# Branch projections run together after the attention, and an output projection with seven of eight half products

## The chip, the cores and the metric

The kernel runs on one core of one Trainium2 chip. The metric is the device time of one execution in microseconds (us). Engines are named as in the profile: PE (TensorE, matmuls), PEld (its weight loads), DVE (VectorE), ACT (ScalarE), POOL (GpSimd) and SP (SyncE, which issues most DMAs). Each engine works its own list in order.

## What is computed

One layer of a streaming encoder on T = 1152 tokens (1024 of a prompt, 128 of eight running streams). An input projection feeds an mLSTM branch and an attention branch. The stretch that is changed is the end of the layer:

```
def merge_out(x, h_m, mz, h_a, az, gm, ga, w_bm, w_ba, w_out):
    u_m = jnp.einsum("btc,cd->btd", h_m * jax.nn.silu(mz), w_bm)
    u_a = jnp.einsum("btc,cd->btd", h_a * jax.nn.silu(az), w_ba)
    mix = jax.nn.sigmoid(gm) * u_m + jax.nn.sigmoid(ga) * u_a
    return x + jnp.einsum("btd,de->bte", mix, w_out)
```

`h_m` and `h_a` are 512 wide, `mix` and the output 1024 wide. All of it is float32.

## The kernel before

Activations lie feature by token: 128 features on the partitions, tokens along the free axis. A float32 product is made of three fp32r matmuls: an operand is split into `hi` (ACT copies it, rounding) and `lo` (the rest, by a subtraction on DVE or POOL; `split`, L98 to L100), and `mm3` (L113 to L116) adds hi·hi, hi·lo and lo·hi into one bank of PSUM. Every matmul loads its own 128x128 weights. `load_nt` (L102) fetches 128 output features' weights in parts of four 128x128 blocks, 256 KB each, into `wr` (2 buffers), and splits them into `wh` and `wl` (3 buffers each).

A planner (`run_line`) interleaves attention chains with input projection tiles; a compile-time scheduler fixes the order on every engine. When the tiles run out, `um_work` does the mLSTM branch: `load_ops` brings `h_m·silu(mz)` back from DRAM (`hm_sc`) into rows 0 to 3 of `h_hi` and `h_lo`, which held the layer's input; then eight output tiles of three chunks of 384 tokens, 12 matmuls each, into `pmain` (2 banks). Their evacuation (`um_evac`) loads the gate from `tg_sc`, multiplies on DVE and stores to `sm_sc`. `load_ops(o_sc, 4)` then fills rows 4 to 7 with the attention's output. The branch from `w_ba` follows, again eight tiles of three chunks (6 banks): DVE multiplies by the gate, POOL adds the stored mLSTM part (L982), and the sum is split into `x_hi` and `x_lo`. At last eight output tiles of three chunks, 24 matmuls each, are added to x (L995) and stored. The three stages have 288, 288 and 576 matmuls of 384 columns.

Of the kernel before, what the change touches and what calls it, by code (L numbers as in the profile page):

```python
# [26 lines left out]
KSC = float(P ** -0.5)  # L27


def emit(tc, a, o, ctx):  # L30
# [930 lines left out]
    load_ops(o_sc, 4)  # L961
# [10 lines left out]
    for j in range(8):

        sa = f(wq_.tile([P, KD, CH], F32R, tag=("w_hi", "w_lo")[j % 2], name="sa", bufs=1)).rearrange("p k c -> p (k c)")
        sm, ta = sa[:, 0:T], sa[:, T:2 * T]
        sp.dma_start(sm, sm_sc[j])
        sp.dma_start(ta, tg_sc[8 + j])

        def ev_a(c, ps):
            s = slice(c * CH, (c + 1) * CH)  # L980
# [6 lines left out]
    def x_rhs(k, c):  # L987
        s = slice(c * CH, (c + 1) * CH)
        return x_hi[:, k, s], x_lo[:, k, s]

    for e in range(8):
        def ev(c, ps):
            xr = wq_.tile([P, CH], F32, tag="wqr", name="xr", bufs=4).rearrange("p (i t) -> p i t", i=3)
# [116 lines left out]
```

## Time and profile before

| | us |
|---|---|
| median of 3 runs (1068.13 to 1069.43) | 1068.95 |
| the profiled execution | 1067.38 |
| its span | 1065.6 |
| PE busy in the span | 1052.3 |
| DVE busy | 657.4 |
| ACT busy | 421.4 |
| POOL busy | 242.5 |

A matmul's duration in the trace is longer than the distance to the next one's start, since matmuls overlap in the array; what a stream of matmuls costs is read from the starts. The granted TensorE clock is full in all slices but the last. HBM moved 122 GB/s over the span.

### The profile page before, as it was taken

How to read it: one execution, taken by the hardware profiler on the slowest of the kernel's cores; microseconds unless marked ns; L12 is line 12 of the kernel's file. 1: busy time of each engine (PE TensorE's matmuls, PEld its weight loads, DVE VectorE, ACT ScalarE, POOL GpSimd, SP SyncE). 2: the span in 40 equal slices, each digit the busy share in tenths (PEclk: the TensorE clock that was granted, in tenths of full speed). 3: DMA queues.
4: the chain of work that ended last, by engine and by line, in shares of the span. 5: the costliest groups of instructions: out<-in, count | busy, mean ns of one | idle time of the engine just before them, and what ended most of it. 6: DMA issues, size and time to landing. Idle time of an engine off the chain costs nothing.

```text
span 1065.6 us, 19714 instructions
## 1 busy us (share of the span) xinstructions
PE 1052.3 (99%) x7078; PEld 1023.0 (96%) x7078; DVE 657.4 (62%) x1931; ACT 421.4 (40%) x976; POOL 242.5 (23%) x406
## 2 busy tenths in 40 slices
PE   7999999999999999999999999999999999999998
PEld 6999999999999999999999999999999999999998
DVE  6745234856747678877877788878753253664221
ACT  6443343344443224654455545545454330231100
POOL 3000000201102234333433344334322000351000
PEclk9999999999999999999999999999999999999999
DMA  8544333452634353423342244123322388663442
GB/s 225 172 90 80 123 49 65 90 119 78 121 105 147 122 181 125 138 67 99 127 139 76 84 132 147 48 83 123 112 87 82 112 267 248 190 221 116 142 139 67
DMA packets 115664, 131.58 MB, mean 123 GB/s; under 512 B 28197, under 2 KB 91885, under 8 KB 115566
## 3 DMA queue, kind: packets, MB, share of 16 engines
q1 hardware_dynamic: 108654, 120.88, 39.6%
q10 hardware_dynamic: 6912, 9.44, 2.4%
q8 instruction: 56, 0.92, 0.4%
q14 instruction: 42, 0.34, 0.1%
HBM read 96.84 MB, written 33.44 MB: 122 GB/s over the span
## 4 chain that ended last, share of the span: by engine, by line
PE 88%; DMA 5%; DVE 4%; issue 1%; ACT 1%; POOL 1%; SPq 0%; DVEq 0%; POOLq 0%; ACTq 0%
PE pm L114 24%; PE pm L116 23%; PE pm L115 23%; PE pT L571 3%; PE pv L733 3%; DMA sm_sc<-tm 1%; PE pS L703 1%; PE pS L704 1%; DMA xt<-in_x 1%; PE pv L817 1%; PE pv L115 1%; PE pv L116 1%; PE pv L114 1%; DMA V<-v_sc 1%; PE pS L792 1%
## 5 line engine op out<-in xcount | busy, mean ns | idle before, releaser
L114 PE MATMUL pm<-h_hi,wh 128*128 128x384 f32 x1056 | 357.3, 339 | 1.9 <-DVE tm L905 1.1
L116 PE MATMUL pm<-h_hi,wl 128*128 128x384 f32 x1056 | 357.6, 339 | 0.0
L115 PE MATMUL pm<-h_lo,wh 128*128 128x384 f32 x1056 | 357.0, 338 | 0.0
L114 PEld LDWEIGHTS pm<-h_hi,wh 128*128 128x128 f32 x1056 | 198.4, 188 | 6.2 <-issue 3.1
L116 PEld LDWEIGHTS pm<-h_hi,wl 128*128 128x128 f32 x1056 | 198.4, 188 | 1.5
L115 PEld LDWEIGHTS pm<-h_lo,wh 128*128 128x128 f32 x1056 | 198.5, 188 | 0.6
L99 ACT ACTIVATE wh<-wr 128x512 fp32r<-128x512 f32 x104 | 65.1, 628 | 166.6 <-PE pm L115 142.2
L114 PE MATMUL pm<-w_hi,h_hi 128*128 128x384 f32 (+1 forms) x360 | 121.1, 337 | 3.1 <-ACT h_hi L99 1.8
L116 PE MATMUL pm<-w_hi,h_lo 128*128 128x384 f32 (+1 forms) x360 | 119.0, 332 | 1.2 <-DVE h_lo L100 1.2
L115 PE MATMUL pm<-w_lo,h_hi 128*128 128x384 f32 (+1 forms) x360 | 118.8, 331 | 0.0
L100 DVE TENSOR_TENSOR wl<-wr,wh 128x512 fp32r<-128x512 f32 x100 | 76.9, 769 | 67.6 <-ACT wh L99 67.5
L563 ACT ACTIVATE prob<-prob,mx 128x640 f32<-128x640 f32 (+4 forms) x72 | 51.2, 711 | 85.6 <-DVE mx L562 63.6
L565 POOL TENSOR_SCALAR prob<-prob,mx 128x640 f32<-128x640 f32 (+4 forms) x72 | 50.7, 704 | 149.0 <-DVE mx L564 88.1
L114 PEld LDWEIGHTS pm<-w_hi,h_hi 128*128 128x128 f32 x360 | 68.3, 190 | 7.7 <-issue 4.1
L116 PEld LDWEIGHTS pm<-w_hi,h_lo 128*128 128x128 f32 x360 | 68.0, 189 | 2.7 <-DVE h_lo L100 1.7
L115 PEld LDWEIGHTS pm<-w_lo,h_hi 128*128 128x128 f32 x360 | 68.2, 190 | 0.1
L114 PE MATMUL pm<-x_hi,wh 128*128 128x384 f32 x192 | 65.0, 339 | 0.0
L116 PE MATMUL pm<-x_hi,wl 128*128 128x384 f32 x192 | 65.0, 339 | 0.0
L115 PE MATMUL pm<-x_lo,wh 128*128 128x384 f32 x192 | 65.0, 338 | 0.0
L560 DVE CUSTOM_DVE_ANT_0 prob<-pS,bias 128x640 f32<-128x640 f32 (+4 forms) x64 | 41.8, 653 | 17.2 <-PE pT L571 8.6
L982 POOL TENSOR_TENSOR sa<-sa 128x384 f32<-128x384 f32 x24 | 27.7, 1163 | 108.3 <-DVE sa L981 108.3
L995 DVE SCALAR_TENSOR_TENSOR xr<-pm,xr 128x384 f32<-128x384 f32 x24 | 13.4, 558 | 59.4 <-PE pm L116 59.4
(220 smaller groups left out, 1782.1 us busy)
## 6 DMA issues: line engine op xcount, KB each, us to landing
wr<-in_wn SPq DMA_DIRECT2D x72, 256.0 KB, 3.0
tg_sc<-tg SPq DMA_DIRECT2D x48, 192.0 KB, 1.9
kr<-in_Kc SPq DMA_DIRECT2D x16, 512.0 KB, 5.3
vr<-in_Vc SPq DMA_DIRECT2D x16, 512.0 KB, 5.2
wqr<-in_wq SPq DMA_DIRECT2D x32, 192.0 KB, 3.3
xt<-in_x SPq DMA_DIRECT2D x9, 512.0 KB, 5.5
tm<-tg_sc SPq DMA_DIRECT2D x24, 192.0 KB, 2.9
sa<-tg_sc SPq DMA_DIRECT2D x8, 576.0 KB, 5.2
```

The source lines that it names most:

```text
L99: act.activation(out=hi, in_=raw, func=AF.Copy)
L100: eng.tensor_tensor(out=lo, in0=raw, in1=f(hi), op=ALU.subtract)
L114: mm(ps, lhs[0], rhs[0], start=first, stop=False)
L115: mm(ps, lhs[0], rhs[1], start=False, stop=False)
L116: mm(ps, lhs[1], rhs[0], start=False, stop=last)
L560: dve.tensor_tensor_reduce(out=view, in0=pS, in1=bias, scale=1.0, scalar=-3e38, op0=ALU.add, op1=ALU.max, accum_out=mx[:, 0:1])
L563: act.activation(out=pt[:, :nk], in_=pt[:, :nk], func=AF.Exp, bias=mx[:, 1:2], accum_out=mx[:, 2:3])
L565: pool.tensor_scalar(out=pt[:, :nk], in0=pt[:, :nk], scalar1=mx[:, 3:4], scalar2=1.0, op0=ALU.mult, op1=ALU.mult)
L571: pe.transpose(pT[:, n * P:(n + 1) * P], pt[:, n * P:(n + 1) * P], ident)
L733: mm(pv[:, j * 256:(j + 1) * 256], at("Vst")[:, i + 1 - nb + n, j, :], st[:, n].rearrange("p a q -> p (a q)"), start=n == 0, stop=n == nb - 1)
L982: pool.tensor_tensor(out=sm[:, s], in0=sm[:, s], in1=ta[:, s], op=ALU.add)
L995: dve.scalar_tensor_tensor(out=xr, in0=ps.rearrange("p (i t) -> p i t", i=3), scalar=0.5, in1=xr, op0=ALU.mult, op1=ALU.add)
```

## The change

The mLSTM branch leaves the planner. Once the planner is done, both operands are loaded by quarters of 288 tokens (`HC`; a half `HF` is 576), part s = 0 of both halves first, then s = 1. For each s and each of four steps `jj`, the two branches are made for output features `jj` and `jj + 4` and both halves: four tiles of `w_bm` weights and products into `pmain`, then of `w_ba` into six banks, eight products of 12 matmuls a step. There is no `sm_sc` any more. `lo` of the weights is made on POOL. From the four results r11, r21, r12, r22 (feature half, token half) the step makes seven operands, x11, x22, x12 and four sums, and splits each.

The output projection takes output tiles in pairs. The weights of a pair are four blocks, b11, b12, b21, b22, from which seven operands are made as well. Seven products of 4·3 matmuls for each s give four blocks of outputs (Winograd's form), where eight would be needed directly. The three running sums of a part stand in three PSUM banks. Split weights lie in columns of `h_hi` and `h_lo` that the s = 1 products have read; four of the s = 1 operands in columns that the s = 0 products have read. Matmuls in the three stages: 384, 384 and 672, of 288 columns.

```diff
@@ -880,31 +883,14 @@
-    def um_work():
-        load_ops(hm_sc, 0)
-        for j in range(8):
-            w = load_nt(a["wbm"][j], 4)
-            for c in range(NCH):
-                yield from chunk(c, w, h_rhs, um_evac(j), 4)
...
+    def load_ops(src, k0, s):
+        for half in range(2):
+            t = slice(half * HF + s * HC, half * HF + (s + 1) * HC)
...
-            t_ = wq_.tile([P, CH], F32, tag="wqr", name="tm", bufs=4)
-            sp.dma_start(t_, tg_sc[j][:, s])
-            dve.scalar_tensor_tensor(out=t_, in0=t_, scalar=1.0, in1=ps, op0=ALU.add, op1=ALU.mult)
-            act.dma_start(sm_sc[j][:, s], t_)
-        return ev
+                raw = spl.tile([P, 1024], F32, tag="kvr", name="raw", bufs=4)[:, 0:2 * HC].rearrange("p (k t) -> p k t", k=2)
+                sp.dma_start(raw, src[kk:kk + 2, :, t].rearrange("k p t -> p k t"))
+                split(h_hi[:, k0 + kk:k0 + kk + 2, t], h_lo[:, k0 + kk:k0 + kk + 2, t], raw)
...
-            if not did and not work and ums is not None:
-                if next(ums, "end") == "end":
-                    ums = None
-                else:
-                    line.now += 480
-                did = True
...
-    load_ops(o_sc, 4)
+    for s in range(2):
+        load_ops(hm_sc, 0, s)
+        load_ops(o_sc, 4, s)
...
-    for j in range(8):
-        sa = f(wq_.tile([P, KD, CH], F32R, tag=("w_hi", "w_lo")[j % 2], name="sa", bufs=1)).rearrange("p k c -> p (k c)")
-        sm, ta = sa[:, 0:T], sa[:, T:2 * T]
-        sp.dma_start(sm, sm_sc[j])
-        sp.dma_start(ta, tg_sc[8 + j])
-        def ev_a(c, ps):
-            s = slice(c * CH, (c + 1) * CH)
-            dve.scalar_tensor_tensor(out=ta[:, s], in0=ta[:, s], scalar=1.0, in1=ps, op0=ALU.add, op1=ALU.mult)
-            pool.tensor_tensor(out=sm[:, s], in0=sm[:, s], in1=ta[:, s], op=ALU.add)
-            split(x_hi[:, j, s], x_lo[:, j, s], sm[:, s])
-        feature_tile(load_nt(a["wba"][j], 4), lambda k, c: h_rhs(4 + k, c), ev_a, 4, pp, "pu")
...
-        def ev(c, ps):
-            xr = wq_.tile([P, CH], F32, tag="wqr", name="xr", bufs=4).rearrange("p (i t) -> p i t", i=3)
-            sp.dma_start(xr, a["xT"][3 * c:3 * c + 3, :, e, :].rearrange("i p t -> p i t"))
-            dve.scalar_tensor_tensor(out=xr, in0=ps.rearrange("p (i t) -> p i t", i=3), scalar=0.5, in1=xr, op0=ALU.mult, op1=ALU.add)
-            act.dma_start(o["y"][e][:, c * CH:(c + 1) * CH], xr.rearrange("p i t -> p (i t)"))
-        feature_tile(load_nt(a["wout"][e]), x_rhs, ev, KD, pp, "pu")
...
+    names = ("x11", "S1", "x12", "S2", "S4", "S3", "x22")
+    X_ = {}
+    for s in range(2):
+        for q, n_ in enumerate(names):
+            if s == 1 and q < 4:
+                k0, t0 = KH * (q // 2), HF * (q % 2)
+                X_[n_, s] = [t_[:, k0:k0 + KH, t0:t0 + HC] for t_ in (h_hi, h_lo)]
+            else:
+                X_[n_, s] = [fp.tile([P, KH, HC], F32R, name=f"{n_}_{s}_{r_}") for r_ in ("hi", "lo")]
...
+        return pp.tile([P, 512], F32, tag="b" + "350214"[(Bank.n - 1) % 6], name="pu")[:, :HC]
+    def branch(ps, w, k0, half, s):
+        t = slice(half * HF + s * HC, half * HF + (s + 1) * HC)
+        for k in range(KH):
+            mm3(ps, w[k], (h_hi[:, k0 + k, t], h_lo[:, k0 + k, t]), k == 0, k == KH - 1)
+    for s in range(2):
+        c = slice(s * HC, (s + 1) * HC)
+        for jj in range(KH):
+            tm, ta = ([sap.tile([P, 2, HC], F32, tag=f"{t_}{e}", name=t_, bufs=2 if t_ == "tm" else 1) for e in range(2)] for t_ in ("tm", "ta"))
+            for t_, j0, e in ((tm, 0, 1), (tm, 0, 0), (ta, 8, 0), (ta, 8, 1)):
+                sp.dma_start(t_[e], tg_sc[j0 + jj + KH * e].rearrange("p (h t) -> p h t", h=2)[:, :, c])
+            for e in (1, 0):
+                w = load_nt(a["wbm"][jj + KH * e], 4, eng=pool)
+                for half in range(2):
+                    ps = pmain.tile([P, 512], F32, tag="pm", name="pm")[:, :HC]
+                    branch(ps, w, 0, half, s)
+                    x = tm[e][:, half, :]
+                    dve.scalar_tensor_tensor(out=x, in0=x, scalar=1.0, in1=ps, op0=ALU.add, op1=ALU.mult)
+            r = {}
+            for e in (0, 1):
+                w = load_nt(a["wba"][jj + KH * e], 4, eng=pool)
+                for half in ((0, 1) if e == 0 else (1, 0)):
+                    ps = bank()
+                    branch(ps, w, KH, half, s)
+                    x, t_ = tm[e][:, half, :], ta[e][:, half, :]
+                    if e:
+                        dve.scalar_tensor_tensor(out=ps, in0=t_, scalar=1.0, in1=ps, op0=ALU.add, op1=ALU.mult)
+                        dve.tensor_tensor(out=ps, in0=ps, in1=x, op=ALU.add)
+                        r[half] = ps
+                    else:
+                        dve.scalar_tensor_tensor(out=t_, in0=t_, scalar=1.0, in1=ps, op0=ALU.add, op1=ALU.mult)
+                        pool.tensor_tensor(out=x, in0=x, in1=t_, op=ALU.add)
+            r11, r21, r12, r22 = tm[0][:, 0, :], tm[0][:, 1, :], r[0], r[1]
+            t3, t2 = (stg.tile([P, CH], F32, tag="th", name=n_)[:, :HC] for n_ in ("t3", "t2"))
+            def put(n_, raw, eng=dve):
+                q = X_[n_, s]
+                split(q[0][:, jj, :], q[1][:, jj, :], raw, eng)
+            put("x11", r11, pool)
+            pool.tensor_tensor(out=t3, in0=r11, in1=r21, op=ALU.subtract)
+            put("S3", t3, pool)
+            put("x22", r22)
+            dve.tensor_tensor(out=r22, in0=r22, in1=r21, op=ALU.add)
+            put("S1", r22)
+            dve.tensor_tensor(out=t2, in0=r22, in1=r11, op=ALU.subtract)
+            put("x12", r12)
+            dve.tensor_tensor(out=r12, in0=r12, in1=t2, op=ALU.subtract)
+            put("S4", r12)
+            put("S2", t2, pool)
+    views = [[t_[:, k0:k0 + KH, t0:t0 + P] for t_ in (h_hi, h_lo)] for k0 in (0, KH) for t0 in (HC, HC + P, HF + HC, HF + HC + P)]
...
+    def w_raw():
+        raws[0] += 1
+        q = raws[0] % 5
+        if q in (1, 4):
+            return wp.tile([P, 4, P], F32, tag="wr", bufs=2, name="wr").rearrange("p k c -> p (k c)")
+        return sap.tile([P, 512 if q == 2 else 2 * HC], F32, tag={2: "wr", 3: "ta0", 0: "ta1"}[q], name="wr", bufs=1)[:, 0:512]
+    def product(ps, w, x, first):
+        for k in range(KH):
+            for l, r in ((0, 0), (0, 1), (1, 0)):
+                mm(ps, w[l][:, k, :], x[r][:, k, :], start=first and k + l + r == 0, stop=k == KH - 1 and l == 1, skip_group_check=True)
...
+        def halves(x):
+            hi, lo = views[parts[0] % len(views)]
+            parts[0] += 1
+            split(hi, lo, x.rearrange("p (k c) -> p k c", k=KH))
+            return hi, lo
...
+        w = {}
+        b11, b12 = load(n1, 0), load(n2, 0)
+        w[1] = halves(b11)
+        b21, b22 = load(n1, 1), load(n2, 1)
+        sub(b11, b12, b11)
+        w[5] = halves(b11)
+        w[2] = halves(b21)
+        t2 = w_raw()
+        sub(t2, b22, b11)
+        w[6] = halves(t2)
+        w[3] = halves(b22)
+        sub(b12, b22, b12)
+        w[7] = halves(b12)
+        sub(b21, b21, t2)
+        w[4] = halves(b21)
+        def steps(s):
+            X, W, Z = (pp.tile([P, 512], F32, tag=banks[2 * q + s], name="py")[:, :HC] for q in range(3))
+            (p1, t_), (u2, xr) = ([t[:, q, :] for q in range(2)] for t in (sap.tile([P, 2, HC], F32, tag=n_, name=n_) for n_ in ("tm0", "tm1")))
+            product(X, w[1], X_["x11", s], True)
+            act.activation(out=p1, in_=X, func=AF.Copy)
+            yield
+            product(W, w[5], X_["S1", s], True)
+            act.activation(out=t_, in_=W, func=AF.Copy)
+            pool.tensor_tensor(out=t_, in0=p1, in1=t_, op=ALU.add)
+            yield
+            product(X, w[2], X_["x12", s], False)
+            out(0, 0, s, X)
+            yield
+            product(Z, w[6], X_["S2", s], True)
+            add(dve, u2, Z, p1)
+            yield
+            product(W, w[3], X_["S4", s], False)
+            add(dve, u2, W, u2)
+            out(1, 0, s, u2)
+            yield
+            product(Z, w[7], X_["S3", s], False)
+            add(dve, t_, Z, t_)
+            out(1, 1, s, t_, xr)
+            yield
+            product(Z, w[4], X_["x22", s], False)
+            add(dve, p1, Z, p1)
+            out(0, 1, s, p1)
...
+    for n1 in range(0, 8, 2):
+        s0, s1 = out_pair(n1, n1 + 1)
+        next(s0)
+        if left:
+            next(left, None)
+        order = (s0,) * 5 + (s1, s0) + (s1,) * 5 if n1 < 6 else (s0, s0) + (s1, s0) * 4 + (s1,) * 5
+        for th in order:
+            next(th, None)
+        left = s1
+    next(left, None)
...
-    d["xT"] = c(xa.reshape(NT, P, KD, P).transpose(0, 3, 2, 1))
+    d["xT"] = c(xa.T).reshape(KD, P, T)
```

PE, where the last gate tile (`pm_10433`) ends and the branches begin. Before:

```order
L116 MATMUL pm_10433<-h_hi_89,wl_10374 128x384
L114 MATMUL pm_10491<-h_hi_89,wh_10487 128x384
L115 MATMUL pm_10491<-h_lo_90,wh_10487 128x384
L116 MATMUL pm_10491<-h_hi_89,wl_10488 128x384
...
L116 MATMUL pm_10491<-h_hi_89,wl_10488 128x384
L114 MATMUL pm_10508<-h_hi_89,wh_10487 128x384
L115 MATMUL pm_10508<-h_lo_90,wh_10487 128x384
L116 MATMUL pm_10508<-h_hi_89,wl_10488 128x384
```

and now (`pm` is the product of `w_bm`, `pu` that of `w_ba`; line numbers are three higher):

```order
L119 MATMUL pm_10433<-h_hi_89,wl_10374 128x384
L117 MATMUL pm_10573<-h_hi_89,wh_10569 128x288
L118 MATMUL pm_10573<-h_lo_90,wh_10569 128x288
L119 MATMUL pm_10573<-h_hi_89,wl_10570 128x288
...
L119 MATMUL pm_10573<-h_hi_89,wl_10570 128x288
L117 MATMUL pu_10641<-h_hi_89,wh_10637 128x288
L118 MATMUL pu_10641<-h_lo_90,wh_10637 128x288
L117 MATMUL pu_10656<-h_hi_89,wh_10637 128x288
L118 MATMUL pu_10656<-h_lo_90,wh_10637 128x288
L117 MATMUL pm_10587<-h_hi_89,wh_10569 128x288
...
L119 MATMUL pu_10641<-h_hi_89,wl_10638 128x288
```

Before, the next 12 matmuls use the same weights `wh_10487`. Now four matmuls on the attention's operand, with weights `wh_10637`, stand between the first and the second product of `w_bm`, and the rest of the product `pu_10641` comes after the second.

ACT at the same place (`tg` is a gate's evacuation, `raw` a loaded piece of an operand). Before:

```order
L201 ACTIVATE tg_10402<-pm_10377,bh_88 128x384
L99 ACTIVATE h_hi_89<-raw_10469 128x2x384
L99 ACTIVATE h_hi_89<-raw_10473 128x2x384
L201 ACTIVATE tg_10430<-pm_10405,bh_88 128x384
L99 ACTIVATE h_hi_89<-raw_10477 128x2x384
L99 ACTIVATE h_hi_89<-raw_10941 128x2x384
L99 ACTIVATE wh_10544<-wr_10542 128x512
L99 ACTIVATE h_hi_89<-raw_10481 128x2x384
L99 ACTIVATE h_hi_89<-raw_10945 128x2x384
L99 ACTIVATE wh_10601<-wr_10599 128x512
L201 ACTIVATE tg_10458<-pm_10433,bh_88 128x384
```

and now:

```order
L204 ACTIVATE tg_10402<-pm_10377,bh_88 128x384
L102 ACTIVATE h_hi_89<-raw_10477 128x2x288
L102 ACTIVATE h_hi_89<-raw_10481 128x2x288
L204 ACTIVATE tg_10430<-pm_10405,bh_88 128x384
L102 ACTIVATE h_hi_89<-raw_10469 128x2x288
L102 ACTIVATE wh_10603<-wr_10601 128x512
L102 ACTIVATE h_hi_89<-raw_10473 128x2x288
L102 ACTIVATE h_hi_89<-raw_10485 128x2x288
L102 ACTIVATE wh_10637<-wr_10635 128x512
L204 ACTIVATE tg_10458<-pm_10433,bh_88 128x384
L102 ACTIVATE h_hi_89<-raw_10489 128x2x288
```

Before, six pieces of the attention's output and of `h_m` are mixed, with the two next weights ahead of the last gate `tg_10458`. Now the piece `raw_10485`, the seventh to be loaded into four buffers, stands ahead of the weights `wh_10637` and of `tg_10458`.

POOL after the attention. Before (the last row of the attention and the first tiles of the `w_ba` stage):

```order
L747 TENSOR_TENSOR ot_10119<-ot_10119,za_4167 128x128
L982 TENSOR_TENSOR sa_10977<-sa_10977 128x384 x3
L982 TENSOR_TENSOR sa_11037<-sa_11037 128x384 x3
L982 TENSOR_TENSOR sa_11097<-sa_11097 128x384 x3
L982 TENSOR_TENSOR sa_11157<-sa_11157 128x384 x3
```

and now, in the first two steps (`L1012` adds the branches, `L1021` is r11 - r21, `L103` makes the `lo` of weights and operands):

```order
L1012 TENSOR_TENSOR tm_10559<-tm_10559,ta_10561 128x288
L103 TENSOR_TENSOR wl_10738<-wr_10735,wh_10737 128x512
L1012 TENSOR_TENSOR tm_10559<-tm_10559,ta_10561 128x288
L103 TENSOR_TENSOR wl_10772<-wr_10769,wh_10771 128x512
L1021 TENSOR_TENSOR t3_10707<-tm_10559 128x288
L103 TENSOR_TENSOR x11_0_lo_10540<-tm_10559,x11_0_hi_10539 128x288
L103 TENSOR_TENSOR wl_10806<-wr_10803,wh_10805 128x512
L103 TENSOR_TENSOR S3_0_lo_10550<-t3_10707,S3_0_hi_10549 128x288
L103 TENSOR_TENSOR wl_10842<-wr_10839,wh_10841 128x512
L103 TENSOR_TENSOR S2_0_lo_10546<-t2_10708,S2_0_hi_10545 128x288
```

Before, POOL has three additions a tile and nothing else. Now each step gives it four `lo` of weights and six operations on operands, in one list.

## Rows read from the trace of the kernel before

**Rows 1.** The page: busy time by engine, and the chain that ended last by engine.
```profile
PE 1052.3 (99%) x7078; PEld 1023.0 (96%) x7078; DVE 657.4 (62%) x1931; ACT 421.4 (40%) x976; POOL 242.5 (23%) x406
...
PE 88%; DMA 5%; DVE 4%; issue 1%; ACT 1%; POOL 1%; SPq 0%; DVEq 0%; POOLq 0%; ACTq 0%
```

**Rows 2.** Busy time by stretch; the header names the columns.
```profile
core 0: us, PE busy (x) PEld busy (x) DVE busy (x) ACT busy (x) POOL busy (x), PEclk, DMA share, GB/s
857.46:865.00 7.54, 6.80 (x39) 6.48 (x39) 6.64 (x9) 5.13 (x8) 0.00 (x0) 1.00 0.90 260
865.00:886.00 21.00, 19.92 (x112) 18.93 (x111) 8.52 (x14) 3.22 (x6) 0.00 (x0) 1.00 0.84 279
886.00:960.28 74.28, 74.28 (x431) 74.28 (x429) 42.15 (x66) 17.64 (x33) 24.26 (x21) 1.00 0.67 214
960.28:1062.20 101.92, 101.92 (x577) 101.59 (x576) 26.80 (x44) 10.31 (x17) 3.44 (x3) 1.00 0.37 117
```

**Rows 3.** Timeline of PE at the first branch products: start, duration, instruction, [idle before].
```profile
857.46 0.33 PE L114 MATMUL pm<-h_hi,wh 128*128 128x384 f32 x1
...
860.44 0.45 PE L114 MATMUL pm<-h_hi,wh 128*128 128x384 f32 x1 [0.74 <-ACT tg L201]
```

**Rows 4.** Timeline of the last microseconds, PE and DVE.
```profile
1061.86 0.34 PE L116 MATMUL pm<-x_hi,wl 128*128 128x384 f32 x1
...
1062.24 0.56 DVE L995 SCALAR_TENSOR_TENSOR xr<-pm,xr 128x384 f32<-128x384 f32 x1 [3.68 <-PE pm L116]
```

**Rows 5.** Timeline of PE: first and last starts of three unbroken streams.
```profile
27.10 0.28 PE L114 MATMUL pm<-w_hi,h_hi 128*128 128x264 f32 x1
...
31.11 0.28 PE L114 MATMUL pm<-w_hi,h_hi 128*128 128x264 f32 x1
...
774.51 0.31 PE L703 MATMUL pS<-Kst,q_hi 128*128 128x320 f32 x1
...
774.95 0.31 PE L704 MATMUL pS<-Kst,q_lo 128*128 128x320 f32 x1
...
886.44 0.33 PE L114 MATMUL pm<-h_hi,wh 128*128 128x384 f32 x1
...
899.96 0.33 PE L114 MATMUL pm<-h_hi,wh 128*128 128x384 f32 x1
```

**Rows 6.** Operand loads: timelines of SP and ACT, and the loads' time to landing.
```profile
848.08 1.41 SPq L896 DMA_DIRECT2D raw<-hm_sc  x2
...
854.54 0.85 ACT L99 ACTIVATE h_hi<-raw 128x768 fp32r<-128x768 f32 x1 [0.41 <-PE pm L116]
856.57 0.85 ACT L99 ACTIVATE h_hi<-raw 128x768 fp32r<-128x768 f32 x1 [1.18 <-DMA raw<-o_sc]
...
DMA to landing us min/median/max: 4.2/4.5/5.9
```

**Rows 7.** POOL: additions L982 (min/median/max ns), and two subtractions by form.
```profile
L982 POOL TENSOR_TENSOR sa<-sa x24: 1004/1207/1517, 908.0 to 964.2; 128x384 f32<-128x384 f32 x24
...
L100 POOL TENSOR_TENSOR w_lo<-wqr,w_hi 128x264 fp32r<-128x264 f32 x8 | 5.8, 748 | 13.0 <-ACT w_hi L99 12.9
...
L100 POOL TENSOR_TENSOR wl<-wr,wh 128x512 fp32r<-128x512 f32 x4 | 5.1, 1291 | 9.0 <-ACT wh L99 9.0
```

**Rows 8.** Groups by form, DVE and ACT: busy us, mean ns of one | idle before.
```profile
L100 DVE TENSOR_TENSOR wl<-wr,wh 128x512 fp32r<-128x512 f32 x100 | 76.9, 769 | 67.6 <-ACT wh L99 67.5
L100 DVE TENSOR_TENSOR x_lo<-sa,x_hi 128x384 fp32r<-128x384 f32 x24 | 15.5, 647 | 7.8 <-ACT x_hi L99 7.7
L905 DVE SCALAR_TENSOR_TENSOR tm<-tm,pm 128x384 f32<-128x384 f32 x24 | 13.3, 553 | 28.9 <-DMA tm<-tg_sc 11.8 <-PE pm L116 11.6 <-DMA sm_sc<-tm 3.2
...
L99 ACT ACTIVATE wh<-wr 128x512 fp32r<-128x512 f32 x104 | 65.1, 628 | 166.6 <-PE pm L115 142.2 <-DMA tm<-tg_sc 7.1 <-DMA wr<-in_wbm 6.2
```

**Rows 9.** DMA issues from 830 us: count, KB each, median us to landing.
```profile
wr<-in_wbm SPq DMA_DIRECT2D x8, 256.0 KB, 5.1
wr<-in_wba SPq DMA_DIRECT2D x8, 256.0 KB, 3.5
```

More of the change, by code (lines that the diff above doesn't have):

```diff
@@ L27 @@
 KSC = float(P ** -0.5)
+HF = T // 2
+HC = HF // 2
+KH = KD // 2
 def emit(tc, a, o, ctx):
@@ L915, in run_line @@
         pairs = pair_work()
-        ums = um_work()
         work = {"pairs": pairs, "tiles": tile_work()}
@@ L947, in run_line @@
                         break
-            if not did and not work and ums is not None:
-                if next(ums, "end") == "end":
-                    ums = None
-                else:
-                    line.now += 480
-                did = True
             if not did:
-                if not live and not samples and not work and ums is None:
+                if not live and not samples and not work:
                     break
@@ L987, in x_rhs @@
[L987 to L992, printed above, removed]
-            xr = wq_.tile([P, CH], F32, tag="wqr", name="xr", bufs=4).rearrange("p (i t) -> p i t", i=3)
-            sp.dma_start(xr, a["xT"][3 * c:3 * c + 3, :, e, :].rearrange("i p t -> p i t"))
-            dve.scalar_tensor_tensor(out=xr, in0=ps.rearrange("p (i t) -> p i t", i=3), scalar=0.5, in1=xr, op0=ALU.mult, op1=ALU.add)
-            act.dma_start(o["y"][e][:, c * CH:(c + 1) * CH], xr.rearrange("p i t -> p (i t)"))
-        feature_tile(load_nt(a["wout"][e]), x_rhs, ev, KD, pp, "pu")
+    esQ.close()
@@ new lines, in emit @@
+    esA, sap = open_pool("sa", bufs=2, side="right")
+    esF, fp = open_pool("fin", side="right")
+    esPS, pp = open_pool("pF", space=PSUM)
+    names = ("x11", "S1", "x12", "S2", "S4", "S3", "x22")
[7 more added lines that the diff above has]
+                X_[n_, s] = [fp.tile([P, KH, HC], F32R, name=f"{n_}_{s}_{r_}") for r_ in ("hi", "lo")]
@@ new lines, in emit, with bank @@
+    banks = [f"b{q}" for q in range(6)]
+    class Bank:
+        n = 0
+    def bank():
+        Bank.n += 1
+        return pp.tile([P, 512], F32, tag="b" + "350214"[(Bank.n - 1) % 6], name="pu")[:, :HC]
[46 more added lines that the diff above has]
+            put("S2", t2, pool)
@@ new lines, in add, with out_pair, load, sub @@
+    def add(eng, out, x, y):
+        eng.tensor_tensor(out=out, in0=x, in1=y, op=ALU.add)
+    def out_pair(n1, n2):
+        def load(n, q):
+            t_ = w_raw()
+            sp.dma_start(t_, a["wout"][n][:, KH * q:KH * q + KH, :].rearrange("p k c -> p (k c)"))
+            return t_
+        def halves(x):
[3 more added lines that the diff above has]
+            return hi, lo
+        def sub(out, x, y):
+            pool.tensor_tensor(out=out, in0=x, in1=y, op=ALU.subtract)
+        def out(e, half, s, x, xr=None):
+            n, c = (n1, n2)[e], slice(half * HF + s * HC, half * HF + (s + 1) * HC)
+            if xr is None:
+                outs[0] += 1
+                q = outs[0] % 3
+                xr = stg.tile([P, CH], F32, tag="gz" if q == 2 else "th", name="xr", bufs=1 if q == 2 else 2)[:, :HC]
+            sp.dma_start(xr, a["xT"][n][:, c])
+            dve.scalar_tensor_tensor(out=xr, in0=x, scalar=0.5, in1=xr, op0=ALU.mult, op1=ALU.add)
+            act.dma_start(o["y"][n][:, c], xr)
+        w = {}
[40 more added lines that the diff above has]
+            out(0, 1, s, p1)
+        return steps(0), steps(1)
@@ L999, in emit @@
+    left = None
+    for n1 in range(0, 8, 2):
[8 more added lines that the diff above has]
+    next(left, None)
     esPS.close()
     esF.close()
-    esQ.close()
+    esA.close()
 def layout(x):
```

14 lines of the change are left out of this document (2 added, 12 removed).

## The prediction

> **What bounds the kernel.** I read the page first. PE is busy for 1052.3 us, 99% of the span, and the chain that ended last is 88% PE [rows 1]: time goes away only if PE has less to do, or comes back as gaps on PE. The windows come next, with the change's place cut out by stages [rows 2]. In the timeline the first `w_bm` matmul starts at 857.46 [rows 3] and the last of all at 1061.86 [rows 4]; with one matmul's distance it is done at 1062.04, 204.6 us later. On PE's list nothing ahead of 857.46 is changed. The granted clock is 1.00 in all four windows, 2.4 GHz.
>
> The stretch has 1152 matmuls of 384 columns. In the `w_ba` stage 78 start-to-start distances take 899.96 - 886.44 = 13.52 us, .1733 each [rows 5]. The output window has 577 in 101.92, .1766 each, and no idle time. The two branches take 960.28 - 857.46 = 102.82 for 576 (99.8 at .1733), so they lose 3.0; of it (7.54 - 6.80) + (21.00 - 19.92) = 1.82 shows as idle PE [rows 2], the rest as slower starts around the gaps. So today's stretch is nearly dense too.
>
> **What the change does to PE.** There are 384 + 384 + 672 = 1440 matmuls of 288 columns: 1440 x 288 = 414,720 columns for 442,368, 6.25% fewer, yet 288 instructions more. The distance at 288 isn't in the trace. Its neighbours are .1215 at 264 (4.01 us over 33) and .1733 at 384 [rows 5]; the line between them gives .1319. Scaling the output window's .1766 by 288/384 gives .1325, and that I take, since it holds the small losses of a real stage. Low bound: .130, proportional to .1733. High bound: .134, a little above 264's .1215 scaled by 288/264 (.1326). (The 320-column products, .147, are three distances of a short burst, for a rival.) PE then needs 187.2, 190.8 or 193.0 us, against 204.6 now: 13.8 us less before any wait.
>
> **What is removed and added on other engines.** The mLSTM part is no longer stored and loaded back, but each branch weight now comes twice, 32 tiles for 16. A branch step, 96 x .1325 = 12.7 us of PE, brings four weight tiles of 256 KB and four gate tiles of 295 KB, 2.2 MB or 174 GB/s, less than the 214 of 886 to 960 [rows 2]. POOL gets, per step, four `lo` of weights at 1.29 and six operations of 288 columns. For these, 264 columns take .748 and the quickest 384-column addition 1.004 [rows 7], so .80; together 10.0 us. A 384-column addition took 1.207 in the median; if all ran 20% longer POOL would need 12.0, still under 12.7. DVE has 13 operations a step with PSUM or two operands at about .45 (three quarters of .553, and a little) and four `lo` of operands at .49 (three quarters of .647) [rows 8], 7.8 us. ACT has four `hi` of weights at .63 and seven of operands below that, at most 6.9. No engine but PE fills a step. Cover for POOL's work is the next weights being wanted a step later; it is thin, and a rival below.
>
> In the output stage a pair is 168 matmuls, 22.3 us. DVE makes seven `lo` of weights (7 x .77) and some 16 operations of about .45, 12.6; POOL some 7. Both hide.
>
> **The waits that it adds on PE**, in order of place.
>
> *The start, 3.0.* The second group on PE needs `wh_10637`, the first `w_ba` weights. On ACT these stand behind `raw_10485`, the seventh piece into four buffers. Its load can go out only when the split of the piece that held its buffer before, `raw_10469`, is done. ACT's copy of that one stands right behind the gate `tg_10430`, as the copy at 854.54 does now [rows 6]; it takes .64 (three quarters of .85), and DVE's `lo` after it ends near 856.1. Such loads need 4.2 to 5.9 to land [rows 6], so 860.3 to 862.0; `hi` .65 and `wh` .63 [rows 8] make 861.4 to 863.1. PE has one product, 12 x .1325 = 1.6, from 857.46 to 859.05: it waits 2.4 to 4.1. I take 3.0. Behind ACT's wait stand the gate `tg_10458` and the later copies, which nobody wants sooner. Now PE loses .74 at the like place [rows 3].
>
> *The next loads, .7.* The pieces for s = 1 and two more weights pass through the same SP queue in the first step, where today's windows move 260 and 279 GB/s [rows 2]. Below: 0; above: the 1.8 that idles now.
>
> *Branch to output, .5.* Of the first pair's four weight blocks the third (b21) goes into the place of a gate (`ta0`) that is free only after POOL's last addition from it, and lands, at 3.5 [rows 9], 2.5 to 3.3 us into the output stage. With its copy and `lo` it is ready at about 4.8 to 5; PE first does three products, 4.75, so 0 to .5.
>
> *The last pair, .8.* Its final two products share one bank. The last can begin when DVE has added the one before (about .45 and the signalling); everywhere else another part's product fills that place.
>
> *Slow starts after gaps, 1.2*, as 3.0 - 1.82 today.
>
> **The sum.** 857.46 + 190.8 + 3.0 + .7 + .5 + .8 + 1.2 = 1054.5, against 1062.04: -7.6. Behind the last matmul comes today one DVE operation of .56 [rows 4] and a store; then two, the shorter one each, +.3. So -7.3 on a profiled execution of 1067.38, which is 1.57 below the median: 1060.1 there, **1061.6 as a median**. By the bounds (-3.6 and +2.2 on the matmuls, -1.5 and +1.5 on the waits) 1056.5 to 1065.3.
>
> **The rivals.**
>
> *Waits that hide (.12).* The matmuls run proportionally and half the waits vanish: -3.6 - 2: 1055 to 1058. For it: ACT and DVE have time. Against: the output window has no gap and still runs at .1766.
>
> *Late weights, mild (.13).* Only two buffers take raw weights. The second `w_ba` tile of a step can be issued only when the `lo` of a tile two earlier is done on POOL, at best 8.3 us into the step; with .7 for its predecessor's copy ahead of it, 1.3 for that `lo`, 3.5 landing and signalling [rows 9], and .7, it is there at 14.7 counted from the step's start, and PE wants it at 12.7 + 3.2 = 15.8: 1.1 to spare. At 5.1, as `w_bm` loads take at 260 to 279 GB/s, it is .5 late, and so is the following step's first: 1 us a step, seven steps, +7, 1065 to 1071, with 1068.6 at its middle. Against: the stage asks for 174 GB/s, and at 214 landing was 3.5.
>
> *Late weights, severe (.07): slower.* The same place: the delay grows by 2 x 7 = 14 us per us of landing beyond 4.6. At 5.1 the saving of 7.3 is gone; from 5.27 the kernel is slower by more than 2.1 us. The longest landing seen, 5.9 [rows 6], gives +18, 1080. POOL slowed as its longest addition (1517 for 1004 [rows 7]) acts alike: 10.0 x 1.5 = 15 us a step for 12.7, +2.3 in each of eight steps, 1080. The Trainium skill, "GPSIMD Engine Reference", section "1. Specifications", says that GpSimd shares its interfaces to SBUF with VectorE. The spread of POOL's additions agrees; in the new stage most of DVE's operations read PSUM, which speaks for less of it.
>
> *A fixed cost per matmul (.03): slower.* If much of the .1733 did not shrink with the columns, more and shorter matmuls would cost time: the saving ends at (204.6 - 6.5) / 1440 = .1376. At 320's .147 [rows 5] PE would need 211.7, +20.9, 1082. The 33 distances of .1215 at 264 columns, with the same three forms and weight loads, nearly rule it out. The Trainium skill, "TensorE: Matmul & The Clock Gate", section "Back-to-back issue gap", gives some 81 ns at 128 columns and 131 at 512 for pairs of weight load and matmul; an estimate by it would be 102 at 288 and 114 at 384, hence 146.7 us for 131.6, a loss of 15 us. Rows 5 show distances that go with the columns, and the measurement decides.
>
> *Something unseen (.05)*, half of it on either side: the start costs 6 or more, or the scheduler's order starves PE in the output stage (the weights' `lo` and the evacuations are in one DVE list).
>
> **Chances.** My own case, 1058 to 1065.5, has .60. What a measurement of this kernel tells from no change is .2%, 2.1 us: below 1066.8 is faster, above 1071.1 slower. Faster: .60 + .12 + .05 of the mild case + .02 = .79. Same: .08 + .01 = .09. Slower: .07 + .03 + .02 = .12. The range leaves out the ends: 1056 to 1070.
>
> **What the profile will show.** Matmul starts .1325 apart in dense pieces of both stages (.130 or .134 at the bounds; .14 or more is the fixed cost). One gap of 2.4 to 4.1 near 859, ended by ACT's `wh`. Eight steps in 101.8 plus about 5, so the output stage from about 965; its end at 1054 to 1055. In the steps, gaps on PE ahead of a first matmul of a weight tile, ended by `wh` or `wl`, mean late weights; then POOL's share of a step or the landing of `wr` says which of the two. A long row of DVE releases in the output stage means that the sharing of banks costs more than the one .8. I am wrong above all if POOL's `lo` of weights take 1.7 or more, or the loads land above 4.6.

## The result, and the profile after

The changed kernel takes 1059.76 us (median of 4 runs, 1058.85 to 1062.8), before 1069.19: a ratio of .9918, interval .9895 to .994, so 9.4 us less. Five more runs of the same kernel (`e0_again`) gave 1060.77 beside 1069.12 for before, ratio .992 (.9907 to .9932). Forecast were 1061.6, within 1056 to 1070. The profiled execution took 1058.85, 8.5 less than that of before, where -7.3 was forecast.

The page, first and chain lines, to stand beside [rows 1]:

```profile
PE 1042.3 (99%) x7366; PEld 1012.9 (96%) x7366; DVE 688.0 (65%) x2035; ACT 452.9 (43%) x1056; POOL 324.0 (31%) x486
...
PE 89%; DMA 5%; DVE 3%; ACT 1%; issue 1%; POOL 1%; SPq 0%; POOLq 0%; ACTq 0%; DVEq 0%
```

PE has 10 us less to do with 288 matmuls more. The windows, cut where the branches begin, where the gaps end, and where the output begins (as [rows 2]):

```profile
859.61:880.00 20.39, 19.81 (x148) 19.34 (x148) 16.37 (x31) 12.18 (x23) 13.17 (x12) 1.00 0.82 243
880.00:962.48 82.48, 82.48 (x624) 82.48 (x623) 45.55 (x110) 32.28 (x70) 64.15 (x66) 1.00 0.56 166
962.48:1053.02 90.54, 89.72 (x674) 89.18 (x672) 53.57 (x97) 23.30 (x48) 29.48 (x26) 1.00 0.46 138
```

The branches take 962.48 - 859.61 = 102.87, as before (102.82). The output takes 90.54 for 101.76. The gain is all in the output projection; the stretch is 193.4 for 204.6. Inside the branches two differences cancel: 768 distances of .1327 (below) are 101.9 us, where 576 of .1733 [rows 5] were 99.8, so the same columns cost 2.1 us more, and what is lost in gaps is 1.0 for 3.0.

The timeline of PE: the first matmul, the gaps, the first and last start of the longest unbroken stream, and the last product:

```profile
859.61 0.29 PE L117 MATMUL pm<-h_hi,wh 128*128 128x288 f32 x1
...
875.80 0.40 PE L117 MATMUL pu<-h_hi,wh 128*128 128x288 f32 x1 [0.22 <-ACT wh L102]
...
876.95 0.40 PE L117 MATMUL pm<-h_hi,wh 128*128 128x288 f32 x1 [0.35 <-DVE tm L997]
...
877.44 0.30 PE L117 MATMUL pm<-h_hi,wh 128*128 128x288 f32 x1
...
962.35 0.30 PE L119 MATMUL pu<-h_hi,wl 128*128 128x288 f32 x1
962.48 0.29 PE L1048 MATMUL py<-x_hi,h_hi 128*128 128x288 f32 x1
...
1051.32 0.40 PE L1048 MATMUL py<-x_hi,h_hi 128*128 128x288 f32 x1 [0.62 <-DVE tm L1051]
...
1052.88 0.29 PE L1048 MATMUL py<-x_hi,h_lo 128*128 128x288 f32 x1
```

From 877.44 to 962.35 there are 640 distances: 84.91 / 640 = .1327. One reads the cost of a gap from the starts around it, not from the idle in brackets: 875.28 to 875.80 is .52, so .39 more than a distance, and the next distance is .24.

Ahead of the branches the changed kernel is 2.15 us later (859.61 for 857.46). This part does the same work in both kernels. Two gaps stand there that the first profile of before doesn't have, on instructions that are the same in both:

```profile
235.86 0.44 PE L117 MATMUL pm<-h_hi,wh 128*128 128x384 f32 x1 [0.91 <-ACT go L335]
...
283.91 0.44 PE L119 MATMUL pm<-h_hi,wl 128*128 128x384 f32 x1 [1.04 <-DVE wl L103]
```

The sum, forecast against profile:

| | forecast | profile |
|---|---|---|
| 1440 matmuls | 190.8 (.1325) | 190.9 (.1326) |
| start | 3.0 | 0 |
| next loads | .7 | 1.1 |
| branch to output | .5 | 0 |
| an addition late in the first pair (980.51) | - | .5 |
| last pair | .8 | .9 |
| slow starts | 1.2 | in the lines above |
| stretch | 197.0 | 193.4 |
| behind the last matmul | +.3 | +.5 |
| ahead of the branches | 0 | +2.15 |
| execution | -7.3 | -8.5 |

### The profile page after: what moved, and what is told of

Its sections match the earlier page's. It is cut to its first block, busy times and chain, and to the rows that moved or that the text cites. A ratio compares the mean times of both kernels' runs of the same rounds, so it can differ in the third digit from the quotient of the medians.

```text
span 1057.1 us, 20596 instructions
## 1 busy us (share of the span) xinstructions
PE 1042.3 (99%) x7366; PEld 1012.9 (96%) x7366; DVE 688.0 (65%) x2035; ACT 452.9 (43%) x1056; POOL 324.0 (31%) x486
## 4 chain that ended last, share of the span: by engine, by line
PE 89%; DMA 5%; DVE 3%; ACT 1%; issue 1%; POOL 1%; SPq 0%; POOLq 0%; ACTq 0%; DVEq 0%
PE pm L117 20%; PE pm L119 19%; PE pm L118 19%; PE py L1048 8%; PE pT L574 3%; PE pv L736 3%; PE pu L119 1%; PE pu L118 1%; PE pu L117 1%; PE pS L706 1%; PE pS L707 1%; DMA wr<-in_wn 1%; PE pv L820 1%; DMA V<-v_sc 1%; DMA xt<-in_x 1%
## 5 line engine op out<-in xcount | busy, mean ns | idle before, releaser
L119 PE MATMUL pm<-h_hi,wl 128*128 128x384 f32 (+1 forms) x992 | 331.5, 335 | 1.0 <-DVE wl L103 1.0
L117 PE MATMUL pm<-h_hi,wh 128*128 128x384 f32 (+1 forms) x992 | 331.2, 334 | 1.3 <-ACT go L335 0.9
L118 PE MATMUL pm<-h_lo,wh 128*128 128x384 f32 (+1 forms) x992 | 330.7, 333 | 0.0
L119 PEld LDWEIGHTS pm<-h_hi,wl 128*128 128x128 f32 x992 | 186.3, 188 | 2.7 <-DVE wl L103 1.4
L103 DVE TENSOR_TENSOR wl<-wr,wh 128x512 fp32r<-128x512 f32 x68 | 49.2, 723 | 55.0 <-ACT wh L102 54.8
L103 POOL TENSOR_TENSOR wl<-wr,wh 128x512 fp32r<-128x512 f32 x36 | 47.5, 1320 | 50.7 <-ACT wh L102 50.6
L102 ACT ACTIVATE PT<-pT 128x640 fp32r<-128x640 f32 (+4 forms) x64 | 36.4, 568 | 30.0 <-PE pT L574 29.3
L103 DVE TENSOR_TENSOR PT<-pT,PT 128x640 fp32r<-128x640 f32 (+4 forms) x64 | 41.6, 650 | 5.0 <-ACT PT L102 4.6
L574 PE MATMUL pT<-ident,prob 128*128 128x128 f32 x280 | 43.1, 274 | 0.2
L204 ACT ACTIVATE tg<-pm,bh 128x384 f32<-128x384 f32 x48 | 27.7, 576 | 33.5 <-PE pm L119 16.8
```

The lines of the kernel that those rows point to most:

```text
L102: act.activation(out=hi, in_=raw, func=AF.Copy)
L103: eng.tensor_tensor(out=lo, in0=raw, in1=f(hi), op=ALU.subtract)
L117: mm(ps, lhs[0], rhs[0], start=first, stop=False)
L118: mm(ps, lhs[0], rhs[1], start=False, stop=False)
L119: mm(ps, lhs[1], rhs[0], start=False, stop=last)
L204: act.activation(out=t_, in_=ps, func=AF.Tanh, scale=0.5, bias=bh[:, 20 + j:21 + j])
```

## The experiments

Theory: the time follows the columns multiplied, .1327 us for 288 of them, and what else the change does stays hidden but for the gaps in the table. Rivals: the gain comes from the joined branches or the queues; or the weights are near being late.

**Eight products for seven.** The same tiles, branches and layout of x in DRAM, the output in direct form:

```diff
+            put("S1", r21, pool)
...
-        sub(b11, b12, b11)
-        w[5] = halves(b11)
...
+        for q_, (n, q) in enumerate(((n1, 0), (n1, 1), (n2, 0), (n2, 1))):
+            w[q_] = halves(load(n, q))
...
+            for n_, (ps, w_, half, last) in enumerate(((X, 0, 0, 0), (X, 1, 0, 1), (W, 2, 0, 0), (W, 3, 0, 1), (Z, 0, 1, 0), (Z, 1, 1, 1), (X, 2, 1, 0), (X, 3, 1, 1))):
+                product(ps, w[w_], X_[("x11", "x12", "S1", "x22")[2 * half + last], s], not last)
```

> The output projection takes all eight block products directly, with the same tiles, and only four operands a part are split; the branches stay as in the change. If the saving is columns not multiplied, 96 matmuls more at .1326 us give +12.7 us in the output stage, less up to .9 for the last wait, which falls away: 1071 to 1072.5, a little slower than before. If the saving came from the joined branches or from what was taken off the queues, it stays some 4 to 7 us below the time before. If a matmul had a fixed cost that the distances hide, 1536 matmuls of 288 columns would take over 3 us more than 1152 of 384.

Measured: 1068.21 (10 runs), ratio to before .9995 (.9986 to 1.0005). Windows of branches and output:

```profile
857.27:961.12 103.85, 102.21 (x769) 101.82 (x769) 50.17 (x107) 39.65 (x75) 63.87 (x62) 1.00 0.62 188
961.12:1063.02 101.90, 101.90 (x770) 101.82 (x768) 24.68 (x48) 8.11 (x14) 0.45 (x1) 1.00 0.39 114
```

The output takes 101.90, that is 768 x .1327, and the changed one 90.54: +11.4, the expected 12.7 less the gaps of 1.35 that the changed output has. 1536 matmuls of 288 columns take about as long as 1152 of 384: 101.90 for 101.76 in the output, 103.85 for 102.82 in the branches, where .1327 for .1733 costs 2.1 us more and gaps cost 1.9 for 3.0. So the joined branches and what was taken off the queues give nothing by themselves, and the rival of a fixed cost falls: a matmul costs at most .003 us beyond its share of the columns (three quarters of .1733 are .1300, of the .1766 of the output before .1325). The time is 3 us below the expected 1071; 2.3 of that is the early part, which here starts the branches at 857.27 (below).

**`lo` of the weights made twice.** A step's POOL work goes from 10.0 to 15.3 us:

```diff
             split(wh, wl, wr, eng)
+            if eng is pool:
+                pool.tensor_tensor(out=wl, in0=wr, in1=f(wh), op=ALU.subtract)
```

> POOL makes lo of each branch weight twice, the second time over the first, and PE waits for the second. By the severe rival of the prediction (POOL as the bound) a step needs 10.0 + 4 x 1.32 = 15.3 us of POOL for 12.7 of PE, +2.6 in each of eight steps: about 1080. If POOL's place is not what sets the weights' time, or the cover is wider than a step, less than +5.

Measured: 1095.83, ratio 1.0248, 16 us above the expected 1080. Against the first profile of the changed kernel the branches take 131.05 us (+28.2), the output 95.67 (+5.1), and the part ahead of them is 4.45 longer, where the edit also doubles the `lo` of four weights of the input projection, which go to POOL too (L366). The waits of PE in the branches, us in total, times, longest:

```profile
PE pm L121 <- POOL wl L114: 14.5, 7, 4.6
PE pu L119 <- ACT wh L102: 2.9, 4, 0.9
PE pu L120 <- DVE h_lo L103: 0.8, 1, 0.8
```

With two of .2 they add up to 18.6, close to the 2.6 x 8 = 20.8 worked out for a POOL-bound stage, and 14.5 of them are waits for POOL's `lo`. The other 9.6 are something that I had not priced. Windows around the longest wait:

```profile
878.70:883.40 4.70, 0.17 (x2) 0.00 (x0) 4.38 (x10) 1.93 (x5) 4.70 (x5) 0.87 0.22 51
883.50:886.00 2.50, 2.50 (x10) 2.50 (x11) 1.06 (x3) 1.23 (x3) 2.50 (x3) 0.50 0.92 292
886.00:888.80 2.80, 2.80 (x13) 2.80 (x13) 0.98 (x3) 0.63 (x1) 1.91 (x4) 0.50 0.85 257
889.00:898.00 9.00, 9.00 (x70) 9.00 (x69) 2.83 (x7) 2.26 (x4) 7.47 (x8) 1.00 0.23 58
```

PE stood idle for 4.7 us; then the granted clock is .50, 1.2 GHz, until 888.8, with matmuls .24 apart, and full again after that. Four times in these branches the clock falls so behind a wait; on the matmuls found at .50 some 7 us go that way, and the rest in slow first matmuls behind gaps.

**Each weight loaded twice**, one load behind the other:

```diff
             sp.dma_start(wr, src[:, 4 * q:4 * q + 4, :])
+            if eng is pool:
+                sp.dma_start(wr, src[:, 4 * q:4 * q + 4, :])
```

> Each branch weight is loaded twice, one load after the other into the same buffer, so that its landing takes about 6.5 to 7 us for some 3.3. By the prediction's late-weight rule (14 us for each us of landing beyond 4.6) +27 to +34 us, 1087 to 1094. If the weights had more room than the 1.1 us that I worked out, clearly less, under +15.

Measured: 1097.21, ratio 1.0258, 3 us above the expected range; the branches take 139.9 us, +37. (Four weights of the input projection are loaded twice by this edit too, so its early part is not that of the changed kernel.) PE's waits in the branches add up to 24.0:

```profile
PE pm L119 <- DVE tm L999: 7.0, 5, 2.3
PE pu L119 <- ACT wh L102: 6.5, 6, 1.9
PE pm L121 <- POOL wl L103: 5.7, 7, 1.7
PE pu L121 <- POOL wl L103: 3.1, 7, 0.6
PE pm L119 <- ACT wh L102: 1.7, 1, 1.7
```

One load landed in 2.6 to 2.9 in the median, but SP issues the second only 2.6 to 4.8 us after the first: the 13 pairs in the branches whose landing the trace has took 5.3 to 9.0 from the first issue, 6.9 in the mean, as assumed. By my rule (14 us for each us beyond 4.6) that is 32, for 37 measured. The waits alone are 24.0: 17.0 of them are for `wh` and `wl`, and 7.0 for DVE's evacuation of a bank of `pmain`, which the rule didn't have. Of the other 13, 5.6 are 52 matmuls at a granted clock of .50, and some 8 slow starts behind 29 gaps. So the place is right and the room is small; the price came out near, though by other terms than worked out.

**The last pair in another order.** The seventh product of part 0 goes between the sixth and seventh of part 1:

```diff
-        order = (s0,) * 5 + (s1, s0) + (s1,) * 5 if n1 < 6 else (s0, s0) + (s1, s0) * 4 + (s1,) * 5
+        order = (s0,) * 5 + (s1, s0) + (s1,) * 5 if n1 < 6 else (s0,) + (s1, s0) * 4 + (s1, s1, s0) + (s1,) * 2
```

> In the last pair the seventh product of part 0 is put between the sixth and the seventh of part 1. If the gap of .91 us ahead of the last product is the wait for the addition from the shared bank, it goes: -.8 us, about 1059. If something else is as late there (the weights' lo, a load), the gap stays or moves and the time is the same.

Measured: 1059.74 (6 runs, 1056.93 to 1061.61). The output's window:

```profile
963.83:1053.57 89.74, 89.45 (x674) 89.15 (x672) 53.47 (x97) 23.30 (x48) 29.59 (x26) 1.00 0.45 138
```

89.74 for 90.54: the .8 is there, and no idle time is left at the end. The time doesn't show it, since the early part varies by more: in this profile PE waits 2.64 us at 283.73, and the granted clock is .50 from 283.5 to 286.9.

**Where the gaps of the first two steps come from.** First the changed kernel again:

> The changed kernel once more, unaltered. What comes ahead of the branches is the same work as before the change, so its length (857.5 before, 859.6 in the first profile of the change, 857.3 and 860.5 in two experiments) should fall anywhere between 857 and 861 by chance; the branches and the output should take 102.9 and 90.5 again, the time 1059 to 1060.5. If the change itself delays the early part, the branches start at 859.5 or later again.

Measured: 1060.77, the branches from 860.99 on, 103.7 us, with gaps of 1.9; the output 90.2. The start fits both halves of the expectation, so it decides nothing by itself.

Then `lo` of the weights on DVE, for `w_bm` and `w_ba` alike:

```diff
-                w = load_nt(a["wbm"][jj + KH * e], 4, eng=pool)
+                w = load_nt(a["wbm"][jj + KH * e], 4)
```

> lo of the branch weights on DVE, as before the change. It takes .72 us there for 1.32 on POOL, so a raw buffer comes free .6 sooner and the gaps of the first two steps (1.1 together) shrink by about half: -.5, 1059 to 1059.5. The rival: DVE then has 7.8 + 4 x .72 = 10.7 us a step, its evacuations come later, and PE waits for tm or for bank space: +1 to +4.

Measured: 1061.81, 1 us more than the changed kernel on the same chip (intervals overlap: .9916 to .9943, .9907 to .9932). The gaps are 1.75 in the branches and 2.25 in the output. The waits of PE from the branches on:

```profile
PE pu L117 <- ACT wh L102: 1.3, 1, 1.3
PE py L1048 <- DVE tm L1051: 1.0, 2, 0.6
PE py L1048 <- DVE t L1026: 0.4, 1, 0.4
```

The expectation missed: the wait for the weights' copy is no shorter with the quicker `lo`, and two waits for DVE are worse.

Then a third raw weight buffer in turn with the two:

```diff
+        if turn[0] % 3 == 0:
+            return sap.tile([P, 512], F32, tag="wr", name="wr", bufs=1).rearrange("p (k c) -> p k c", k=4)
+        return wp.tile([P, 4, P], F32, tag="wr", bufs=2, name="wr")
```

> A third raw weight buffer in the branches. If the gaps near 875 come from the w_ba load that could not go out before POOL's lo had freed a buffer, that load starts some 3 us sooner and the 1.1 us of gaps go: about 1058.7. If they come from ACT's order (the operand pieces stand ahead of the weights' copy), the same gaps stay.

Measured: 1059.92. SP issues the `w_ba` load at 866.42 for 871.94, and the wait for `wh` is gone; but the waits of PE are now

```profile
PE pm L120 <- DVE tm L1007: 0.8, 1, 0.8
PE py L1058 <- DVE tm L1061: 0.6, 1, 0.6
```

and the gaps in the branches add up to 1.05. One wait went, and the next in line took its place: a bank of `pmain` is free only after DVE's evacuation, which stands behind the `lo` of the s = 1 pieces and the sums of the step before. This rests on one profile of each kernel.

The third buffer and the other order of the last pair together:

> The third raw buffer and the reordered last pair together: -.8 and -1.1 add, about 1057.9, if the two places have nothing to do with each other.

Measured: 1058.82 (5 runs), ratio .9901 (.9888 to .9915), the lowest median of all, 2 us below the changed kernel beside it; the intervals overlap. The profile gives the last pair its .8 (no gap in the output) and the third buffer nothing (1.57 in the branches). So half the expectation held.

And the s = 1 pieces later, as sixteen loads of one 128x288 block, six at the end of a step, with the other order of the last pair:

```diff
-    for s in range(2):
-        load_ops(hm_sc, 0, s)
-        load_ops(o_sc, 4, s)
+    load_ops(hm_sc, 0, 0)
+    load_ops(o_sc, 4, 0)
...
+            if n_ % 2:
+                raw = stg.tile([P, CH], F32, tag="gz", name="raw", bufs=1)[:, :HC]
+            else:
+                raw = sap.tile([P, 512], F32, tag="wr", name="raw", bufs=1)[:, :HC]
...
+            for _ in range(6):
+                next(late, None)
```

> With the reordered last pair, the operand pieces of s = 1 are loaded one feature block at a time during the first three steps, through two other buffers, and no longer ahead of and within the first step. If the gaps of the first two steps (1.1 to 1.9 us in the profiles so far) come from the crowd of s = 1 pieces on the SP queue, ACT and DVE, they go, about 1058. If other work is as late there, or sixteen small pieces for eight large ones cost as much, they stay or move to later steps.

Measured: 1061.94, ratio .9929 (.9911 to .9947), where the same order of the last pair had .991 and .9901; the intervals overlap, so worse is read from the profile. The branches take 107.0 us: PE waited 2.2 us for `wh` and .6 for `wl` in the first two steps, the granted clock was .50 from 883.2 to 886.6, and gaps and slow matmuls add up to 5.2. That the crowd of s = 1 pieces makes the gaps is not shown; only that this way of thinning it costs more.

**The 2 us ahead of the branches.** Two more profiles of before, and before with 299 tiny operations on DVE, POOL and ACT behind its last store:

> The kernel before once more, for its profile. If the waits of PE near 234 and 282 us, which the profiles of the changed kernel have and that of before has not, are chance in the DMA traffic of the early part, some profiles of before have them too and its branches start at 859 to 861; if the change makes them, the branches start at 857.5 again.

> The kernel before a third time, a second draw for the same question: the branches start at 859 to 861 in some profiles of before if the early waits are chance, and at 857.5 in all of them if the change makes them.

```diff
+            if e == 7 and c == 2:
+                z = xr[:, 0, 0:1]
+                for q in range(120):
+                    dve.tensor_scalar(out=z, in0=z, scalar1=0.5, scalar2=None, op0=ALU.mult)
+                for q in range(93):
+                    pool.tensor_scalar(out=z, in0=z, scalar1=0.5, scalar2=None, op0=ALU.mult)
+                for q in range(86):
+                    act.activation(out=z, in_=z, func=AF.Copy)
```

> The kernel before with 299 tiny operations on one column, on DVE, POOL and ACT, behind the last store: the program is longer by about as many DVE, POOL and ACT instructions as the change adds, and nothing else is different. Only the part ahead of the branches is read. If a longer program by itself makes the early DMAs slower, out_convs takes 9.2 us or more to land and the branches start at 859.5 to 861.7 as in the changed kernels; if not, 7.3 to 8.3 us and 857.3 to 858.6 as in the other profiles of before. A single profile, so a value between the two leaves it open.

The two profiles of before took 1068.68 and 1069.02 in one run each. The padded kernel took 1141.16 as a whole, since its tiny operations run one after another behind the last store; only its early part bears on the question. Start of the branches, landing of the scattered store `out_convs` issued near 222 us, the wait of PE at 282 to 285 us that ends with DVE's `wl`, and the time from one ACT instruction near 174 us to one near 346 us, the same in all kernels:

| | branches start | `out_convs` lands in | wait | 174 to 346 |
|---|---|---|---|---|
| before, three profiles | 857.46, 858.31, 858.60 | 7.6, 8.1, 7.3 | 0, 0, .5 | 171.9, 171.9, 172.5 |
| eight products | 857.27 | 8.3 | 0 | 172.1 |
| changed, and four variants | 859.61, 860.99, 860.51, 859.45, 860.39, 861.71 | 9.3, 9.7, 9.2, 9.3, 9.5, 9.2 | 1.0, 2.4, 2.6, 2.4, 3.1, 3.0 | 174.2, 176.2, 176.4, 175.8, 175.2, 177.2 |
| before, padded | 860.03 | 9.0 | 1.1 | 173.5 |

(The changed kernel stands there twice; the variants are the last pair, the third buffer, both, and `lo` on DVE. The kernel with the later pieces starts its branches at 862.93, with 9.2, 3.2 and 178.2; the two doubled kernels have another early part by their edits.) The six of the changed kernel begin 2.3 us later in the mean than the three of before, and the two groups don't overlap. The two new profiles of before lie between the values that their expectations named (857.5, or 859 to 861). In the first variant (2.6 us of wait) and the last (3.0) the granted clock falls to .50 at this wait (283.5 to 286.9, and 282.0 to 288.9); in the other four it stays full. In the padded kernel the wait is there too:

```profile
284.28 0.45 PE L116 MATMUL pm<-h_hi,wl 128*128 128x384 f32 x1 [1.13 <-DVE wl L100]
```

By the rule set beforehand, its start speaks for the length of the program, and its landing (9.0, where 9.2 was asked) leaves it open. From 174 to 346 us it lies between the groups, and .9 us of its late start stands already at 134 us, as in one profile of before. The eight-product kernel, whose lists on DVE and ACT (1951 and 1004 instructions) are nearer to those of before (1931, 976) than to the changed ones (2035, 1056), with POOL's halfway (446 for 406 and 486), starts the branches early. So the longer lists may make a part of the delay; that they make all of it is not shown, with one padded profile. Nor are the early stores slower throughout: the one near 207 us lands in 10.4 to 10.9 us in before and with eight products, and in 8.6 to 9.2 in the changed and the padded kernels. In its one profile the padding alone thus moves both landings as the change does, one later and one sooner. By which path stays open.

## Why the prediction was right

*The matmuls: right.* .1325 was forecast at 288 columns and .1327 came, in one stream of 640 distances. The scaled output window (.1325) and the interpolation between 264 and 384 columns in [rows 5] (.1319) agree with it. The reason given for taking the first, small losses of a real stage, was not what the traces show: in this stream no distance is above .138, so the price lies in every matmul, and not in gaps. That it holds in the branches too, where before .1733 ran at 384 columns, was lucky; why that stage was 2% quicker for its columns stays open. The Trainium skill's section "Back-to-back issue gap" ("TensorE: Matmul & The Clock Gate"), weighed in the prediction, isn't borne out here: an estimate by it was .102, and .1327 came. `e1_eight` shows the same without the saved products: 33% more matmuls with the same columns take the same time within 1.2 us.

*The start: wrong.* 3.0 were forecast, and nothing is lost. The step that failed is "Its load can go out only when the split of the piece that held its buffer before, `raw_10469`, is done". SP, DVE and ACT:

```profile
854.32 1.98 SPq L892 DMA_DIRECT2D raw<-o_sc  x2
```

```profile
853.54 0.76 DVE L103 TENSOR_TENSOR h_lo<-raw,h_hi 128x576 fp32r<-128x576 f32 x1 [2.65 <-ACT h_hi L102]
```

```profile
852.82 0.69 ACT L102 ACTIVATE h_hi<-raw 128x576 fp32r<-128x576 f32 x1 [0.70 <-DMA raw<-o_sc]
...
856.69 0.69 ACT L102 ACTIVATE h_hi<-raw 128x576 fp32r<-128x576 f32 x1 [0.41 <-PE pm L119]
...
858.09 1.36 ACT L102 ACTIVATE h_hi<-raw 128x576 fp32r<-128x576 f32 x2
859.63 0.63 ACT L102 ACTIVATE wh<-wr 128x512 fp32r<-128x512 f32 x1 [0.18 <-PE pm L118]
```

The load of `raw_10485` goes out at 854.32, ahead of the copy of `raw_10469` at 856.69. It took the buffer of `raw_10477`, which ACT had copied first (852.82) and whose `lo` DVE ended at 854.30. I had taken the buffers in turn, though ACT's order, which stands with the change, splits them in another. `wh_10637` is ready at 860.26, and PE, at 861.19, doesn't wait.

*The next loads: right in place, .7 for 1.1* (1.9 in `e0_again`; the bounds were 0 and 1.8). The cause given, the traffic on the SP queue, isn't shown: with a third raw buffer (`e7_third_raw`) the wait for `wh` goes and one for a bank comes. *Branch to output: 0*, within 0 to .5. *The last pair: .8 for .9*, shown by `e5_last_pair`, which takes it away.

*Other engines.* From 880 to 962.48, 6.5 steps, POOL is busy for 64.15, 9.9 us a step for a forecast of 10.0; the `lo` of a weight took 1.326 and an operand's .80 to .84. "Late weights" did not come: `w_ba` landed in 2.7 and `w_bm` in 3.9, under the 4.6 that I had as the edge. The two doubled kernels show that the edge is real and near: at 6.9 for 4.6 PE lost 37 us in the branches, where the rule gives 32.

*The early part: wrong.* "On PE's list nothing ahead of 857.46 is changed" is true and did not keep its time: +2.15 in the profile, +2.3 in the mean, a term that the sum had at 0. This and what did not come on the stretch (-3.6, of it 3.0 for the start) largely cancel, so it is luck that the sum was closer to the time than its terms.

## What to carry to other kernels

Where PE is busy for 99% of a dense stretch, count columns: an eighth of the products left out gave 11.2 of that stage's 101.8 us, 12.7 less the gaps, though the matmuls there got narrower and were 96 more than before. Who holds a buffer is read from the order in which its users finish, not from the order in which they are written. And a wait removed at a place with several late workers showed the next one here, so look at the second in line ahead of the edit.

## What the runs showed that I had not expected

A wait on PE can cost half as much again behind it: after 4.7 us of idling PE ran at a granted clock of .50 (1.2 GHz) for 5.4 us, and in the two doubled kernels 9.6 of 28.2 us and some 13 of 37 us were not waits, but matmuls at the lower clock and slow first ones behind gaps. After the short gaps of the changed kernel (.2 to .6 us idle) only the one matmul behind the gap was slow, .24 for .13.

And the same early work took 2.3 us more in the mean in the changed kernel, for the most part at a wait near 284 us; 299 instructions behind the end of the kernel before went with 1.4 to 2.6 us more at its branches, in one profile. Two programs should therefore be compared by stages, not only by their totals.
